# Convolution with residual add: weights in front on ACT's queue with the first residual behind them, the first image as one load in front on SP's queue

## The chip, the cores and the metric

One core of a Trainium2 chip. The time is the device time of the program in microseconds (us), a median over executions; the profile's span, some 2 us shorter, runs from the first to the last instruction of one execution. SP and ACT each issue transfers into a queue of their own; the sixteen DMA engines move them in rows, one row per partition. "Packet records" are the trace's list of single rows and semaphore writes, each with start and duration. TensorE is PE, VectorE is DVE, ScalarE is ACT, GpSimd is POOL, SyncE is SP.

## The reference, cut to what matters

```python
batch, c_in, h, w, c_out, k = 16, 64, 64, 64, 64, 3      # all float32
x_pad = np.pad(x, ((0, 0), (0, 0), (1, 1), (1, 1)))
output[b, co] += weight[co, ci, kh, kw] * x_pad[b, ci, kh:kh+h, kw:kw+w]
return output + residual
```

Image and residual are 16.8 MB each, the weights 0.15 MB, the output 16.8 MB: 50.5 MB have to cross between memory and the core.

## The kernel before

Images are handled in pairs: 128 partitions hold two images of 64 channels, so one load of `x`, one of `residual` and one store move 2 MB, in 128 rows of 16 KB. ACT packs each image into bf16 (two copies), PE convolves it, DVE adds the residual in place (two adds), and SP stores the pair. Three buffers hold images, and every residual pair has its own. The weights are transposed by PE, and DVE and ACT copy them, cast to bf16, into the layout that PE uses.

```python
def load_x(p, engine=nc.sync, cols=slice(0, NPIX)):
    return engine.dma_start(out=xr[p % NXR][:, cols], in_=x_bc[128 * p : 128 * p + 128, cols]).then_inc(
        s_x[p % NXR], 16)
...
# SP's program
for p in range(NPAIR):
    if p >= NXR:
        nc.sync.wait_ge(s_half, 2 * (p - NXR) + 3)     # the image buffer is free
    if p == 0:
        to_the_front(load_x(p, cols=slice(0, NPIX // 2)))   # ahead of the start barrier
        nc.sync.dma_start(out=wraw[:, :], in_=w_rows[:, :]).then_inc(s_w, 16)
    else:
        load_x(p)
    load_ro(p)
for p in range(NEARLY):                                # the first 6 stores
    nc.sync.wait_ge(s_add, 2 * p + 3)
    store(p).then_inc(s_out, 16)
...
# ACT's program
to_the_front(load_x(0, nc.scalar, slice(NPIX // 2, NPIX)))
for n in range(B):
    ...                                                # wait for the pair's load, two copies of image n
    if n == 0:
        nc.scalar.wait_ge(s_wt, 1)                     # the transposes
        ...                                            # four weight copies
...
# the last two stores, after everything above is done
for p in range(NEARLY, NPAIR):
    store(p)
```

`to_the_front` moves a load ahead of the barrier with which the program starts.

## Time and profile before

| | before |
|---|---|
| time, median of 3 (range) | 123.16 us (123.14 to 123.23) |
| span of the profiled execution | 121.2 us |
| busy: PE, DVE, ACT | 72%, 63%, 52% |
| moved, mean rate over the span | 50.48 MB, 417 GB/s |

### The profile page before, as it was taken

The page shows a single profiled execution, that of the slowest core. Times are in us where ns is not written, and L with a number is a line of the kernel's source. Part 1 is how long each engine was busy: PE and PEld are TensorE (multiplying, and loading weights), DVE is VectorE, ACT ScalarE, POOL GpSimd, SP SyncE. Part 2 cuts the span into 40 slices and gives each one's busy share as a digit, 9 for nine tenths or more (in the row PEclk, how much of TensorE's full clock was granted, in tenths as well). Part 3 has the DMA queues.
Part 4 walks back from the last instruction along what each step waited for, and adds up shares of the span by engine and source line. Part 5 has one row for each costly group of instructions (what it writes and reads, how often), then busy time and mean ns, then how long its engine had stood idle before and what let it go on. Part 6 is the DMA issues. An engine that isn't in the chain of part 4 may idle for free.

```text
span 121.2 us, 736 instructions
## 1 busy us (share of the span) xinstructions
PE 87.7 (72%) x389; PEld 10.7 (9%) x105; DVE 76.0 (63%) x40; ACT 63.1 (52%) x37; POOL 2.4 (2%) x16
## 2 busy tenths in 40 slices
PE   0033499999999999999999999999999980000000
PEld 0021001101010101010101010101010100000000
DVE  0005300889898898989889898898989889300000
ACT  4049969938966984993993994896000000000000
POOL 5200000000000000000000000000000000000000
PEclk9999999999999999999999999999999999755555
DMA  6999999999999999999999999999999999999993
GB/s 168 427 444 433 433 433 433 433 427 433 433 427 427 433 433 427 427 433 427 433 433 433 433 433 422 433 389 433 433 433 433 422 433 433 433 433 433 427 433 151
DMA packets 3744, 50.48 MB, mean 417 GB/s; under 512 B 416, under 2 KB 544, under 8 KB 544
## 3 DMA queue, kind: packets, MB, share of 16 engines
q1 hardware_dynamic: 3600, 49.43, 96.3%
q10 hardware_dynamic: 144, 1.05, 2.0%
HBM read 33.70 MB, written 16.78 MB: 417 GB/s over the span
## 4 chain that ended last, share of the span: by engine, by line
PE 71%; DVEq 2%; DVE 2%; issue 0%
PE ps L86 53%; PE ps L85 17%; DVEq L129 2%; DVE ro L201 2%
## 5 line engine op out<-in xcount | busy, mean ns | idle before, releaser
L201 DVE TENSOR_TENSOR ro<-ps,ro 64x2048 f32<-64x2048 f32 x32 | 73.2, 2289 | 17.7 <-PE ps L86 17.2
L86 PE MATMUL ps<-xp,wl 128*128 128x504 bf16 (+1 forms) x288 | 80.0, 388 | 0.2
L173 ACT CAST xp<-xr 64x2048 bf16<-64x2048 f32 x16 | 30.3, 1896 | 19.3 <-DMA xr<-in_x_dram 17.1
L85 PE MATMUL ps<-xp,wl 128*128 128x504 bf16 (+1 forms) x92 | 35.8, 389 | 3.4 <-PEq L222 3.4
L177 ACT CAST xp<-xr 64x2048 bf16<-64x2048 f32 x16 | 30.4, 1897 | 0.4
L85 PEld LDWEIGHTS ps<-xp,wl 128*128 128x128 bf16 x96 | 9.5, 99 | 79.1 <-issue 79.1
L189 DVE CAST wl<-ps 32x192 bf16<-32x192 f32 x8 | 2.8, 348 | 10.4 <-PE ps L214 10.3
L214 PE MATMUL ps<-ident,wraw 128*32 128x128 f32 x9 | 2.1, 412 | 8.1 <-DMA wraw<-in_weight_dram 8.1
L214 PEld LDWEIGHTS ps<-ident,wraw 128*32 128x32 f32 x9 | 1.2, 137 | 8.6 <-issue 8.1
L173 ACT ACT_TABLE_LOAD x1 | 1.3, 1283 | 1.1 <-SPq L129 1.1
L182 ACT CAST wl<-ps 32x192 bf16<-32x192 f32 x4 | 1.2, 306 | 0.0
L160 POOL MEMSET xp<- 64x64 bf16 x4 | 0.6, 147 | 0.2
L159 POOL MEMSET xp<- 64x64 bf16 x4 | 0.6, 145 | 0.2
L148 POOL TENSOR_SCALAR_AFFINE_SELECT ident<-ident 128x128 f32<-128x128 f32 x1 | 0.3, 295 | 0.2 <-POOL ident L146 0.2
L162 POOL MEMSET wl<- 64x192 bf16 x1 | 0.3, 253 | 0.1
L161 POOL MEMSET wl<- 64x192 bf16 x1 | 0.3, 252 | 0.1
L146 POOL MEMSET ident<- 128x128 f32 x1 | 0.2, 205 | 0.7 <-SPq L129 0.7
L257 POOL MEMSET const-uint8-127<- 128x1 uint8 x1 | 0.1, 113 | 0.0
L257 POOL MEMSET const-bfloat16-1.0<- 128x1 bf16 x1 | 0.1, 112 | 0.0
L257 POOL MEMSET const-float32-1.0<- 128x1 f32 x1 | 0.1, 109 | 0.0
L257 POOL MEMSET const-float32-0.0<- 128x1 f32 x1 | 0.1, 104 | 0.2 <-issue 0.2
## 6 DMA issues: line engine op xcount, KB each, us to landing
ro<-in_residual_dram SPq DMA_DIRECT2D x8, 2048.0 KB, 21.9
out_dram<-ro SPq DMA_DIRECT2D x8, 2048.0 KB, 28.2
xr<-in_x_dram SPq DMA_DIRECT2D x7, 2048.0 KB, 17.5
xr<-in_x_dram SPq DMA_DIRECT2D x1, 1024.0 KB, 7.0
xr<-in_x_dram ACTq DMA_DIRECT2D x1, 1024.0 KB, 7.6
wraw<-in_weight_dram SPq DMA_DIRECT2D x1, 144.0 KB, 6.9
```

The lines of the kernel that those rows point to most:

```text
L85: return e.matmul(out=out_, lhsT=lhsT, rhs=rhs, start=start, stop=stop, skip_group_check=True)
L86: return e.add_instruction(mybir.InstMatmult(name=nc.get_next_instruction_name(), engine=PE, ins=[e.lower_ap(rhs), e.lower_ap(lhsT)], outs ...
L129: with tc.tile_critical(no_gpsimd_drain=True):
L159: nc.gpsimd.memset(t[0:64, 0, :], 0.0).then_inc(s_id, 1)
L160: nc.gpsimd.memset(t[64:128, J, :], 0.0).then_inc(s_id, 1)
L173: i = nc.scalar.copy(out=t[64:128, 0:J, :], in_=x4[hp, :, 0, :])
L177: nc.scalar.copy(out=t[0:64, 1 : J + 1, :], in_=x4[hp, :, 1, :]).then_inc(s_pack, 1)
L182: i = nc.scalar.copy(**weight_block(h, *b))
L189: i = nc.vector.tensor_copy(**weight_block(h, *b))
L201: i = nc.vector.tensor_tensor(out=o4[hp, :, par, :], in0=psj[64 * par : 64 * par + 64, :, :], in1=o4[hp, :, par, :], op=ADD)
L214: i = nc.tensor.transpose(out=tp[0:32, t // 3, 128 * (t % 3) : 128 * (t % 3) + 128], in_=wraw3[:, :, t], identity=ident[:, :])
L257: nc = _bacc.Bacc("TRN2", target_bir_lowering=False, num_devices=1)
```

## The change

Its visible intent is to have the weights at PE earlier: they go to the front of ACT's program, ACT casts its weight copies before it packs the first image, the image comes as one load at the front of SP's program, and the first residual leaves SP's queue so that the second image moves up there.

```diff
+    def load_w(rows):
+        return nc.scalar.dma_start(out=wraw[rows, :], in_=w_rows[rows, :]).then_inc(s_w, 16)
...
             if p == 0:
-                to_the_front(load_x(p, cols=slice(0, NPIX // 2)))
-                nc.sync.dma_start(out=wraw[:, :], in_=w_rows[:, :]).then_inc(s_w, 16)
+                to_the_front(load_x(p))
             else:
                 load_x(p)
-            load_ro(p)
+            if p > 0:
+                load_ro(p)
...
-        to_the_front(load_x(0, nc.scalar, slice(NPIX // 2, NPIX)))
+        to_the_front(load_w(slice(0, 112)))
+        load_w(slice(112, 128))
+        load_ro(0, nc.scalar)
+        nc.scalar.wait_ge(s_wt, 1)
+        for b in blocks[4:]:
+            for h in range(2):
+                i = nc.scalar.copy(**weight_block(h, *b))
+        i.then_inc(s_wt, 1)
         for n in range(B):
...
-            if n == 0:
-                nc.scalar.wait_ge(s_wt, 1)
-                for b in blocks[4:]:
-                    for h in range(2):
-                        i = nc.scalar.copy(**weight_block(h, *b))
-                i.then_inc(s_wt, 1)
...
-        nc.tensor.wait_ge(s_w, 16)
+        nc.tensor.wait_ge(s_w, 32)
```

(The waits on the first image's semaphore follow from the number of its loads.)

More of the change, by code (lines that the diff above doesn't have):

```diff
@@ L68, with load_x, load_ro @@
     s_add = sem("s_add")
-    def load_x(p, engine=nc.sync, cols=slice(0, NPIX)):
-        return engine.dma_start(out=xr[p % NXR][:, cols], in_=x_bc[128 * p : 128 * p + 128, cols]).then_inc(
-            s_x[p % NXR], 16
-        )
-    def load_ro(p):
-        nc.sync.dma_start(out=ro[p][:, :], in_=res_bc[128 * p : 128 * p + 128, :]).then_inc(s_r[p], 16)
+    def load_w(rows):
+        return nc.scalar.dma_start(out=wraw[rows, :], in_=w_rows[rows, :]).then_inc(s_w, 16)
+    def load_x(p):
+        return nc.sync.dma_start(out=xr[p % NXR][:, :], in_=x_bc[128 * p : 128 * p + 128, :]).then_inc(s_x[p % NXR], 16)
+    def load_ro(p, engine=nc.sync):
+        engine.dma_start(out=ro[p][:, :], in_=res_bc[128 * p : 128 * p + 128, :]).then_inc(s_r[p], 16)
     def store(p):
@@ L171 @@
             if im == 0:
-                nc.scalar.wait_ge(s_x[p % NXR], 16 * (p // NXR + 1 + (p % NXR == 0)))
+                nc.scalar.wait_ge(s_x[p % NXR], 16 * (p // NXR + 1))
             i = nc.scalar.copy(out=t[64:128, 0:J, :], in_=x4[hp, :, 0, :])
```

## The prediction

> **What bounds the kernel now.** I read four views in this order: the page (is any resource full from start to end?), the stages at the end (what runs last?), the start in order of time (what releases the first convolution?), and the transfer queues in a short stretch near the start (how do two queues share?). First the page: engine PE, the sixteen DMA engines and the bytes, then the chain that ended last.
>
> ```profile
> PE   0033499999999999999999999999999980000000
> ...
> DMA  6999999999999999999999999999999999999993
> ...
> HBM read 33.70 MB, written 16.78 MB: 417 GB/s over the span
> ...
> PE 71%; DVEq 2%; DVE 2%; issue 0%
> ```
>
> The DMA row is full in 38 of 40 slices; PE is idle in the last seven. 50.48 MB at the 434 GB/s of an undisturbed stage is 116.3 us of a 121.2 us span. The chain names PE for 71%, but that chain stops at 104 us; it ended 17 us before the span did. So this kernel is bound by the volume it moves, and compute matters only if it makes a transfer queue run empty. The stages at the end, with the columns span, PE, PEld, DVE, ACT, POOL, clock, DMA share and GB/s, and then the last instructions:
>
> ```profile
> 98.00:104.00 6.00, 1.48 (x7) 0.10 (x1) 5.39 (x3) 0.00 (x0) 0.00 (x0) 1.00 1.01 434
> 104.00:110.00 6.00, 0.00 (x0) 0.00 (x0) 0.13 (x1) 0.00 (x0) 0.00 (x0) 0.54 1.02 434
> 110.00:119.00 9.00, 0.00 (x0) 0.00 (x0) 0.00 (x0) 0.00 (x0) 0.00 (x0) 0.50 1.01 431
> 119.00:121.20 2.20, 0.00 (x0) 0.00 (x0) 0.00 (x0) 0.00 (x0) 0.00 (x0) 0.50 0.09 37
> ```
> ```profile
> 99.52 4.61 DVE L201 TENSOR_TENSOR ro<-ps,ro 64x2048 f32<-64x2048 f32 x2 [0.58 <-PE ps L86]
> 104.42 0.96 SPq L79 DMA_DIRECT2D out_dram<-ro  x2
> ```
>
> The last two stores are issued at 104.42 us, right after the last add, while transfers flow at the full rate on both sides of that moment. In the packet records the last 256 rows of 16 KB (those two stores) begin at 109.57 us. So 5.15 us of older work is queued when they are issued. That is the slack of the whole compute chain, less the time from an issue to its first packet. Now the start:
>
> ```profile
> 7.77 1.90 ACT L173 CAST xp<-xr 64x2048 bf16<-64x2048 f32 x1 [5.41 <-DMA xr<-in_x_dram]
> 8.14 2.08 PE L214 MATMUL ps<-ident,wraw 128*32 128x128 f32 x9 [8.14 <-DMA wraw<-in_weight_dram]
> 10.33 2.90 DVE L189 CAST wl<-ps 32x192 bf16<-32x192 f32 x8 [10.33 <-PE ps L214]
> 11.50 1.26 ACT L182 CAST wl<-ps 32x192 bf16<-32x192 f32 x4
> ...
> 13.66 0.59 PE L85 MATMUL ps<-xp,wl 128*128 128x512 bf16 x1 [3.44 <-PEq L222]
> ```
>
> The weights land at about 8.1, are transposed until 10.2, and DVE's casts of them end at 13.23; 0.43 later PE starts. Image 0 is packed by 11.6. The weights, not the image, release the first convolution. From there PE has practically no idle time until 99.5, so the end of compute moves one for one with PE's start.
>
> Last, how the two queues share: the stretch 2.5 to 6.0 us, when SP's half of the first image (q1) and ACT's half (q10) were both queued, and the landing times of the loads (KB each, us from issue to landing):
>
> ```profile
> q10 hardware_dynamic: 92, 0.75, 50.8%
> q1 hardware_dynamic: 89, 0.73, 49.7%
> ```
> ```profile
> xr<-in_x_dram SPq DMA_DIRECT2D x1, 1024.0 KB, 7.0
> xr<-in_x_dram ACTq DMA_DIRECT2D x1, 1024.0 KB, 7.6
> wraw<-in_weight_dram SPq DMA_DIRECT2D x1, 144.0 KB, 6.9
> ```
>
> 92 packets against 89: the queues take turns, one row each. The single records agree: where SP's queue had come to the weights and ACT's still had 8 KB rows, a 51 ns weight row followed each 309 ns row of the image, and the semaphore write that ends a transfer took a turn too. SP's first packet starts at 1.0 us. ACT's first starts only at 2.67 us, although issued at 0.13.
>
> **What the Trainium skill says.** Three places bear on this. "DMA: Bandwidth & Descriptors", section "Issuing engines are not separate DMA queues": DMAs issued from different engines run on the same 16 engines and interleave, and a second issuer saves only issue time. The trace agrees: two active queues share 434 GB/s. The same page, section "Queues, rings and completion order": each DMA engine round-robins between the queue rows at packet granularity, with a packet of typically 9 to 17 descriptors. The round robin is in this trace; the grouping isn't, a turn here is one row. This decides when the weights land. The same page, section "Latency and other measured facts": first byte of this kind of DMA after about 0.6 us. This trace has 1.0 us on SP's queue and 2.5 us on ACT's, and I use those.
>
> **The change part by part.**
>
> *The first image as one load on SP.* The same 2 MB, in 128 rows of 16 KB in place of 256 of 8 KB. A 16 KB row takes 611 ns in the records, two 8 KB rows 618: 7 ns by 8 rows per DMA engine is 0.06 us saved. The cold start may gain a little too: in the first 2.5 us only 38 packets, 0.31 MB, moved, and larger rows carry more behind each slow first answer. I take 0.1 us in all.
>
> *The weights in front on ACT's queue, 112 rows and then 16.* On each DMA engine that is 7 weight rows, a semaphore write, 1 row, a semaphore write: 10 turns. If ACT's queue again wakes at about 2.7, each engine has two 16 KB rows of the image behind it by about 2.9 (the 38 packets at 2.5 are 1.2 such rows per engine). From there every turn costs a 611 ns image row: 0.66 us for a weight row and its image row. Weight row 7 goes at 2.9 + 6 x 0.66 = 6.9; the image's eighth row ends at 6.8; the semaphore write, row 8 and the last semaphore write need two more rows of the next load in between, to 8.2. A semaphore is seen some 0.4 us after its last write (weights before: last writes at 7.6, transposes at 8.1), and the engines are spread by 0.2. So the image is usable at about 7.5 and the weights at about 8.8, that is 0.65 LATER than now, though they stand first in ACT's program.
>
> *ACT's order.* ACT now casts its weight blocks first, then packs image 0. Transposes start at 8.8; 2.19 (8.14 to 10.33) later, at 11.0, the casts begin: 1.26 for four, then 3.83 for the two packs of image 0: 16.1. DVE's eight casts are done at 13.9, hidden. PE starts at about 16.2 instead of 13.66: 2.5 later. This is the real cost of the order: the pack no longer overlaps the transposes.
>
> *The first residual on ACT's queue.* It now takes turns with the second image load instead of going before it. The second image needs 6 more rows after 8.2, each with a residual row: 6 x 2 x 0.61 = 7.3, landing at about 16 (now 17.8); the residual lands at about 18.5 (now 12.4). Its first reader is DVE's first add, at 21.7 now and some 2.5 later then. Both are hidden.
>
> *The end.* Compute ends at 104.1 + 2.5 = 106.6 and the last stores are issued at 106.9. Their first turn comes at about 109.5, so 2.6 us are left for the start of a transfer, which took 1.0 on SP's queue. Still hidden, with 1.6 us to spare. The other waits have more room: the load of the fourth pair is issued at 19.7 now and some 2.1 later then, while the loads queued ahead of it last until about 32.
>
> Sum: bytes unchanged, queue never empty, start and rows -0.1, compute +2.5 but hidden: 123.16 - 0.1 = 123.05 us.
>
> **The rivals.** (1) The weights really come first: if ACT's queue wakes as early as SP's, or turns hold many rows, they land at 3 to 4 us; the transposes then run by 6.3 (GpSimd's constants are ready at 4.1), the image is packed from 7.5 to 11.3, and PE starts at 11.4, 2.3 earlier. That was probably the intent. Against it: ACT's first packet at 2.67 and the one-row turns. It would still give 123.05, as the last transfers don't depend on it. (2) The delay breaks through at the end: if PE starts over 4 us later, or a late store needs the 2.5 us that ACT's first did, the queue empties before the last stores. With my 2.5 us and such a latency nothing is left, so a further 1 us of delay would show as 1 us: 124. For it: the slack is only 5.15. Against it: the stores are on SP's queue, and SP is already running. (3) The kernel is bound by compute and the start counts in full: 120.8 or 125.7. Against it: the empty PE in the last 17 us beside a full DMA row.
>
> **Range and chances.** Runs of the kernel before span 0.09 us. The cold start gives a few tenths either way, rival (2) a tail upward: 122.5 to 123.8. 2% is 2.46 us. Faster needs fewer bytes or a higher rate, neither in the diff: 0.01. Slower needs a delay of some 6.5 us at PE's start: 0.015. Within: 0.975.
>
> **What would show it.** Right: a full DMA row to about 119; the transposes at 8.5 to 9.2; PE's first convolution at 15.5 to 17, released by ACT's pack; the last stores issued near 107 with full DMA after it. Wrong on the turns: transposes before 6. Wrong on the hiding: a dip in GB/s just before the last two stores flow. If the time moves by over 0.7 us without such a dip, the rate itself has changed, and my account of the bound is incomplete.

## The result, and the profile after

The changed kernel took 123.03 us (median of 6 runs, 122.87 to 123.59), the kernel before 123.15 (6 runs, 123.01 to 123.23). The ratio is 1.000, with a 95% interval of 0.998 to 1.002. The two are the same within a quarter of a per cent.

The page of the changed kernel, its rows for PE and the transfers, its bytes and its chain:

```profile
PE   0006039999999999999999999999999999000000
...
DMA  6999999999999999999999999999999999999993
...
HBM read 33.70 MB, written 16.78 MB: 417 GB/s over the span
...
PE 71%; DVEq 2%; DVE 2%; issue 0%
```

Bytes, rate and the full DMA row are as before. PE's row has moved: it is full from the seventh slice on, where before it was from the sixth, and it ends one slice later. The start in order of time shows by how much:

```profile
9.61 2.08 PE L216 MATMUL ps<-ident,wraw 128*32 128x128 f32 x9 [9.61 <-DMA wraw<-in_weight_dram]
11.72 1.26 ACT L172 CAST wl<-ps 32x192 bf16<-32x192 f32 x4 [8.40 <-PE ps L216]
11.80 2.90 DVE L191 CAST wl<-ps 32x192 bf16<-32x192 f32 x8 [11.80 <-PE ps L216]
13.01 1.90 ACT L181 CAST xp<-xr 64x2048 bf16<-64x2048 f32 x1
14.93 1.90 ACT L185 CAST xp<-xr 64x2048 bf16<-64x2048 f32 x1
...
16.97 0.59 PE L86 MATMUL ps<-xp,wl 128*128 128x512 bf16 x1 [5.29 <-PEq L224]
```

The weights start their transposes at 9.61, 1.5 us LATER than before (8.14), and the first convolution starts at 16.97, 3.3 us later (13.66). The pack of image 0 stands behind the weight copies now; before, it ran beside the transposes. At the end that delay is still almost whole (3.2 us), and still hidden. The stages (columns as in the prediction's) and the last two lines of the timeline:

```profile
104.00:110.00 6.00, 0.00 (x0) 0.00 (x0) 3.29 (x2) 0.00 (x0) 0.00 (x0) 0.79 1.02 434
110.00:119.00 9.00, 0.00 (x0) 0.00 (x0) 0.00 (x0) 0.00 (x0) 0.00 (x0) 0.50 1.01 431
```
```profile
102.71 4.61 DVE L203 TENSOR_TENSOR ro<-ps,ro 64x2048 f32<-64x2048 f32 x2 [0.58 <-PE ps L87]
107.61 0.81 SPq L80 DMA_DIRECT2D out_dram<-ro  x2
```

The last stores are issued at 107.61 instead of 104.42. Their first row begins at 109.41 by the packet records, and the rate is 434 GB/s around it, without a dip. So of the 5.15 us between issue and first row, 3.35 were used up and 1.80 are left.

Why the weights came late, although they stand first on their queue, shows in the queues' share between 3.0 and 6.5 us:

```profile
q1 hardware_dynamic: 82, 1.34, 89.6%
q10 hardware_dynamic: 82, 0.09, 7.8%
```

82 packets from each queue, 1.34 MB against 0.09 MB. The queues take turns row by row, and so every weight row of 1152 bytes (51 ns) waited for a row of 16 KB of the image (611 ns).

### The profile page after: what moved, and what is told of

Its sections match the earlier page's. It is cut to its first block, busy times and chain, and to the rows that moved or that the text cites. A ratio compares the mean times of both kernels' runs of the same rounds, so it can differ in the third digit from the quotient of the medians.

```text
span 121.0 us, 736 instructions
## 1 busy us (share of the span) xinstructions
PE 87.6 (72%) x389; PEld 10.7 (9%) x105; DVE 76.0 (63%) x40; ACT 63.2 (52%) x37; POOL 2.4 (2%) x16
## 4 chain that ended last, share of the span: by engine, by line
PE 71%; DVEq 2%; DVE 2%; issue 0%
PE ps L87 54%; PE ps L86 17%; DVEq L130 2%; DVE ro L203 2%
## 6 DMA issues: line engine op xcount, KB each, us to landing
wraw<-in_weight_dram ACTq DMA_DIRECT2D x1, 126.0 KB, 8.2
```

## The experiments

Theory A: the moved bytes, and the moment at which they begin, set the time; compute is hidden as long as the last stores are issued while older transfers still flow. Rival B: the start of the first convolution counts in full. Rival C: row size or the number of queues changes the rate (in the delay runs C stands for a compute chain that can't reach the end at all). All twelve kernels, with the two already shown, in one table. "First row" is the first packet record of the last two stores. All results are correct, except in the two runs with fewer bytes.

| kernel | PE starts | last stores issued | first row | time, median us | ratio to before, 95% |
|---|---|---|---|---|---|
| before | 13.66 | 104.42 | 109.57 | 123.15 | |
| changed | 16.97 | 107.61 | 109.41 | 123.03 | 1.000 (0.998 to 1.002) |
| p1_image_one_load | 13.91 | 104.66 | 109.39 | 123.14 | 0.999 (0.996 to 1.001) |
| p2_weights_first_on_sp | 15.09 | 104.92 | 109.56 | 123.14 | 1.000 (0.997 to 1.002) |
| p3_pack_before_casts | 15.10 | 105.63 | 109.45 | 123.16 | 0.999 (0.997 to 1.002) |
| p4_residual_on_sp | 16.99 | 107.66 | 109.84 | 123.33 | 1.002 (0.998 to 1.006) |
| q1_image_on_act | 14.65 | 105.68 | 109.81 | 123.06 | 0.999 (0.997 to 1.001) |
| p5_image_after_barrier | 13.22 | 104.26 | 110.64 | 124.06 | 1.007 (1.005 to 1.008) |
| d1_delay | 18.87 | 109.80 | 110.63 | 124.01 | 1.005 (1.003 to 1.008) |
| d2_delay | 20.70 | 110.40 | 111.23 | 125.20 | 1.018 (1.014 to 1.022) |
| l0_less_bytes_before | 13.49 | 103.86 | 104.71 | 118.31 | 0.962 (0.960 to 0.964) |
| l1_less_bytes | 16.95 | 106.84 | 107.68 | 121.19 | 0.984 (0.983 to 0.986) |

**One part alone: the image as one load (from the kernel before).**

```diff
-                to_the_front(load_x(p, cols=slice(0, NPIX // 2)))
+                to_the_front(load_x(p))
-        to_the_front(load_x(0, nc.scalar, slice(NPIX // 2, NPIX)))
```

> The kernel before with one part of the change: the first image as one load on SP, nothing on ACT's queue, weights behind the image on SP. Theory A (the moved bytes set the time, the start is hidden behind them): 122.9 to 123.3 us. Theory B (the start of the first convolution counts in full): 123.4, as PE should start at about 13.9 in place of 13.66 (image rows end at about 7.4, weights seen at 8.3, transposes and casts 5.1, 0.43 to PE). Theory C (row size or the number of queues changes the transfer rate): 0.06 us or more below the kernel before, from fewer and larger rows.

Measured: PE starts at 13.91, as expected, and the time doesn't move. An effect of 0.06 us, as rival C would have it, is below what the interval resolves. So this part explains at most 0.25 us of PE's delay (13.91 for 13.66).

**The weights truly first: on SP's queue ahead of the image (from the changed kernel).**

```diff
+                to_the_front(load_w(slice(0, 112)))            # now issued on SP
                 to_the_front(load_x(p))
-            if p > 0:
-                load_ro(p)
+            load_ro(p)
-        to_the_front(load_w(slice(0, 112)))
-        load_w(slice(112, 128))
-        load_ro(0, nc.scalar)
+        load_w(slice(112, 128), nc.scalar)
```

(All 128 rows in one front load, or both pieces in front, does not compile; I don't know why. So 16 rows had to go behind the barrier.)

> The changed kernel with the 112 weight rows ahead of the image on SP's own queue, the other 16 on ACT's, the residual back on SP. The weights should now really come first: transposes at 4.5 to 5 instead of 9.6, image packed from 8.3 to 12.1, PE starts at about 12.2, 4.8 us before the changed kernel. Theory A: time unchanged, 122.8 to 123.3, last stores issued at about 102.9. Theory B: 118.3. If turns on a DMA engine held many rows, the weights would not move by this much, because they would already have come first.

Half a miss. The 112 rows landed 2.2 us after their issue, but the other 16, issued on ACT at 1.44, had their first row only at 5.5 and landed 6.2 us after their issue. The transposes ran at 7.72 instead of 4.5 to 5, and PE started at 15.09. The time stayed the same with PE 1.9 us earlier than in the changed kernel, which speaks against B, but the early start that I wanted was not reached. Two things follow: both pieces must land, and a load issued just behind a large one on the OTHER queue starts late.

**ACT's order undone (from the changed kernel).**

```diff
-        nc.scalar.wait_ge(s_wt, 1)
-        for b in blocks[4:]: ...                 # weight copies ahead of image 0
...
+            if n == 0:                           # behind the pack of image 0, as before the change
+                nc.scalar.wait_ge(s_wt, 1)
+                for b in blocks[4:]: ...
```

> The changed kernel with ACT's order undone: image 0 is packed before ACT casts its weight blocks. Transposes stay at 9.6; the pack should run from 7.9 to 11.7 beside them, DVE's casts end at 14.7, PE starts at 15.1 instead of 16.97. Theory A: time unchanged, 122.8 to 123.4. Theory B: 121.2.

Measured: transposes at 9.58, PE at 15.10, as expected, and the time the same. So of the changed kernel's 3.3 us delay of PE, ACT's order costs 1.9 and the later weights the other 1.4.

**The first residual back on SP (from the changed kernel).**

```diff
-            if p > 0:
-                load_ro(p)
+            load_ro(p)
-        load_ro(0, nc.scalar)
```

> The changed kernel with the first residual back on SP's queue behind the first image; only the weights on ACT. Transposes should stay at 9.6 and PE at 17.0, as the residual does not take a turn before the weights' last one. The first residual lands at about 12.7, the second image at about 17.6 instead of 16.8. Theory A: 122.8 to 123.4. Theory C (sharing two queues costs rate): below the changed kernel by 0.2 or more.

Measured: transposes at 9.62 and PE at 16.99, as in the changed kernel, so the residual has no part in the delay. The time is the same within its interval. C's 0.2 us below the changed kernel did not show (123.33 against 123.03, of different rounds), but an interval of 0.4% either way could not resolve it.

**The front loads exchanged: image on ACT, weights on SP.**

```diff
-                to_the_front(load_x(p))
+                to_the_front(load_w(slice(0, 112)))            # on SP
+                load_w(slice(112, 128))
-        to_the_front(load_w(slice(0, 112)))
-        load_w(slice(112, 128))
+        to_the_front(load_x(0, nc.scalar))
```

> The changed kernel with the two front loads exchanged: 112 weight rows on SP, the first image on ACT, the other 16 weight rows on SP after the barrier. If ACT's queue wakes late by itself (2.7 to 3.0 us in the traces so far), the image's first row starts there and the transfers lose 1 us or more: 124.0 or above. If it was only kept waiting behind the rows that SP had issued first, the image starts right after the weights, at 1.5 to 1.9, and the time is 123.0 to 123.4. PE's start is 15 to 20 either way, as the second image now takes turns with the first.

This was aimed at an assumption of mine, that ACT's queue by itself wakes at about 2.7 us. The queues between 1.0 and 2.5 us, packets, MB and share:

```profile
q10 hardware_dynamic: 19, 0.31, 90.9%
q1 hardware_dynamic: 128, 0.13, 29.1%
```

ACT's queue (q10) had begun 19 image rows by 2.5 us, its first at 1.42 by the packet records. It doesn't wake late by itself; in the kernels before and after it was kept waiting behind the 128 rows that SP had issued 0.13 us earlier. Here it is the 16 weight rows on SP, issued at about 1.1 behind ACT's image, that begin only at 4.78 us. Why a load waits like this for one on the other queue, and for how long, these runs don't show. The time is unchanged (123.06). PE's start at 14.65 lies just outside the 15 to 20 expected.

**The transfers begin later, PE earlier: the image behind the barrier.**

```diff
-                to_the_front(load_x(p))
+                to_the_front(load_w(slice(0, 112)))            # on SP
+                load_w(slice(112, 128))
+                load_x(p)
-            if p > 0:
-                load_ro(p)
+            load_ro(p)
-        to_the_front(load_w(slice(0, 112)))
-        load_w(slice(112, 128))
-        load_ro(0, nc.scalar)
```

> The changed kernel with all on SP: 112 weight rows in front, then after the start barrier the other 16, the first image, the first residual. Weights are seen by 3, transposes run when GpSimd's constants are ready, 4.1 to 6.2; the image is packed from 8.9 to 12.7, PE starts at about 12.9, 4.1 us before the changed kernel. But the large transfers begin about 1.4 us later, 0.35 of which the weights fill. Theory A (moved bytes and the moment they begin set the time): 123.6 to 124.2, SLOWER though PE starts earlier. Theory B (start of compute counts): 118.9.

The stages of this kernel from 1 to 3 us and one line of its timeline:

```profile
1.00:2.00 1.00, 0.00 (x0) 0.00 (x0) 0.00 (x0) 1.00 (x1) 0.65 (x4) 1.00 0.52 134
2.00:3.00 1.00, 0.00 (x0) 0.00 (x0) 0.00 (x0) 0.25 (x1) 0.73 (x6) 1.00 1.17 243
```
```profile
4.01 2.10 PE L214 MATMUL ps<-ident,wraw 128*32 128x128 f32 x9 [4.01 <-POOL wl L164]
```

The transposes now wait for GpSimd's constants (4.01), not for the weights, and PE starts at 13.22, earlier than in any other full kernel. Yet the time is 124.06, up by 0.7%: the DMA engines are half idle until 2 us, and between 1 and 4 us they moved 0.3 MB less than in the changed kernel (134, 243 and 197 GB/s against 246, 280 and 350), an estimated 0.7 us at 434 GB/s. B would have 119, and is refuted by the sign of the change. A's 123.6 to 124.2 held.

**More delay, one and two copies of 1.9 us ahead of the first pack (from the changed kernel).**

```diff
+            for k in range(1 if n == 0 else 0):                # 2 in the second kernel
+                nc.scalar.copy(out=t[64:128, 0:J, :], in_=x4[hp, :, 0, :]).then_inc(s_slow, 1)
+                nc.scalar.wait_ge(s_slow, k + 1)
             i = nc.scalar.copy(out=t[64:128, 0:J, :], in_=x4[hp, :, 0, :])
```

> The changed kernel with one more copy of 1.9 us on ACT ahead of the first pack: PE starts at 18.9 instead of 16.97, the last stores are issued at 109.55 instead of 107.61. The queued transfers end between 109.4 and 110.2, so the slack of 1.8 us is used up. Theory A (only what goes past the slack shows): the rise is 1.9 - (1.8 - L), with L the time from an issue to its first row on a running SP queue; with L of 1.0 as at the start, 1.1 us, about 124.1; with L near 2, 125. Theory B (all of compute counts): 1.9 us, 124.9. Theory C (compute does not touch the end at all): 123.0. The last rows should begin after a hole in the transfers of about L.

> The same with two such copies: PE starts at 20.9, last stores issued at 111.45. Theory A: once the slack is gone every further microsecond counts in full, 1.9 above the run with one copy: about 126.0 with L of 1.0. Theory B: 126.8. Theory C: 123.0.

The kernel with one copy at the end, stages and last issue:

```profile
107.00:109.50 2.50, 0.00 (x0) 0.00 (x0) 2.47 (x2) 0.00 (x0) 0.00 (x0) 1.00 0.96 413
109.50:110.60 1.10, 0.00 (x0) 0.00 (x0) 0.00 (x1) 0.00 (x0) 0.00 (x0) 0.72 0.01 0
110.60:112.00 1.40, 0.00 (x0) 0.00 (x0) 0.00 (x0) 0.00 (x0) 0.00 (x0) 0.50 1.34 562
```
```profile
109.80 0.81 SPq L81 DMA_DIRECT2D out_dram<-ro  x2
```

This is the hole that the changed kernel just avoids: the queue has run empty, the stores are issued at 109.80, and their first row comes at 110.63, 0.83 later. The time rose to 124.01, near A's 124.1; against the 123.21 of the kernel before in the same rounds the rise is 0.3 to 1.0 us by the interval, a little under A's 1.1, and clear of B's 1.9 and of C's none. With two copies the latency is 0.83 again (110.40 to 111.23) and the hole longer. So the slack that the changed kernel had left in its profiled execution is 1.80 - 0.83 = 0.97 us.

The second run missed its number: 125.2 instead of 126.0, with runs from 124.5 to 126.0. The profiled execution (124.52) was the fastest of its four. In it PE started 1.83 us later than with one copy but ended only 0.6 later. The reason is in PE's first groups of four matmuls, which go at 1.7 us each before they settle at 0.87. The first matmul of the first group at the shorter time, with one copy and then with two:

```profile
25.16 0.38 PE L87 MATMUL ps<-xp,wl 128*128 128x504 bf16 x1
```
```profile
24.03 0.38 PE L87 MATMUL ps<-xp,wl 128*128 128x504 bf16 x1
```

In the profile with two copies that slow phase lasted 3.3 us, in the one with a single copy 5.8, and in the changed kernel 5.2 (from PE's first convolution to the trace's first record of the full clock). Half of the 2.5 us between the first two is the 1.2 that PE caught up. The Trainium skill, "TensorE: Matmul & The Clock Gate", section "Part 1: The HAM clock gate (the "warmup" mystery)", describes such a phase after idleness and says that its length differs from run to run, as the window that PE's activity is measured in runs freely. The traces agree that the length varies: it was 3.3 to 6.0 us over the twelve profiles, and PE's time from first to last convolution varied with it by 1.3 us (84.8 to 86.1). So PE's end, and the slack at the end with it, can differ by about that much for this reason alone. With one trace per kernel, its spread between executions of the same kernel is not shown, nor that it made the other runs of the two kernels slower or faster.

**Fewer bytes: the last residual pair not loaded, in both kernels (the edit to the kernel before; in the changed kernel the condition is `0 < p < NPAIR - 1`).**

```diff
-            load_ro(p)
+            if p < NPAIR - 1:
+                load_ro(p)
+        nc.gpsimd.wait_ge(s_id, 4 + 2 * NXP)
+        nc.gpsimd.memset(ro[NPAIR - 1][:, :], 0.0).then_inc(s_r[NPAIR - 1], 16)
```

> The kernel before, wrong on purpose: the last residual pair is not loaded (GpSimd writes zeros instead), so 2.1 MB or 4.86 us of transfers less. The last stores are still issued at about 104.4; their rows can begin 0.83 later (the delay runs gave 0.83 from issue to first row), at 105.3, in place of 109.57. Theory A: 4.3 us less, 118.9. If the bytes alone counted: 118.3. Theory B (compute counts in full): unchanged, 123.2.

> The changed kernel with the same cut. The last stores are issued at about 107.6, so their rows begin at 108.4 in place of 109.41. Theory A: only 1.0 us less, 122.0, that is 3.1 us or 2.6% slower than the kernel before with the same cut: the 3.2 us of later compute that are hidden in the full kernels show. If the bytes alone counted: 118.2, equal to the other.

Stages near the end of the kernel before, and then of the changed kernel, both without that load:

```profile
103.00:105.00 2.00, 0.00 (x0) 0.00 (x0) 0.56 (x1) 0.00 (x0) 0.00 (x0) 0.62 1.04 442
105.00:107.60 2.60, 0.00 (x0) 0.00 (x0) 0.00 (x0) 0.00 (x0) 0.00 (x0) 0.50 0.95 403
```
```profile
103.00:105.00 2.00, 0.00 (x0) 0.00 (x0) 1.97 (x2) 0.00 (x0) 0.00 (x0) 1.00 0.75 320
105.00:107.60 2.60, 0.00 (x0) 0.00 (x0) 1.55 (x1) 0.00 (x0) 0.00 (x0) 0.69 0.00 0
```

With 4.86 us of transfers less, the kernel before gained 4.8 us (118.31 against 123.08 of the same rounds): bytes set its time. The changed kernel gained only 1.9 (121.19), because its transfers stand still from about 105 to 107.6, until the last stores can be issued. Between these two the changed arrangement is 2.9 us, 2.4% by the medians, slower. Both beat A's own numbers, 118.9 and 122.0, by 0.6 and 0.8: the last stores were issued at 103.86 and 106.84 instead of the 104.4 and 107.6 assumed. In the second kernel PE starts at 16.95, as in the changed kernel, but its slow phase lasted 3.7 us instead of 5.2, and half of that difference is the 0.8. So the delay of PE's start is real and reaches the end; in the full kernels it lies behind queued transfers. This also shows the limit of "bytes set the time": it holds for the kernel before with a margin of 4.3 us (5.15 - 0.83), and for the changed kernel with one of 1.0, both as profiled and so give or take the slow phase of PE.

No version beat the kernel before. The intervals of p1, p2, p3, p4 and q1 all contain 1.

## Why the prediction was right

*The bound.* Right. The transfers fill the same 38 slices, and the time stayed within 0.12 us while PE's start moved by 3.3. Taking bytes away moved the time nearly in full (118.31), and starting the transfers later raised it even with PE earlier (124.06).

*The turns.* Right in kind: one row each (82 to 82), and the weights came later, not earlier, as the prediction said against the change's visible intent. The size was off. The transposes began at 9.61, not 8.8, and outside the 8.5 to 9.2 that I had named. Two terms were too small: the last semaphore writes of the weights were spread over 0.7 us between the DMA engines (8.28 to 8.96 in the packet records) where 0.2 had been allowed; and the last was seen 0.65 later, not 0.4 (the two times that it was taken from differ by 0.5). The first of them came as worked out (8.2). The spread could have been read from the kernel before, where it is 0.6 (7.06 to 7.66). That it comes from the first rows of 16 KB, which took 1.0 to 1.7 us each, is likely but not shown. The second image and the first residual landed at 16.7 and 19.2 for 16 and 18.5, late by as much, and hidden as said.

*The cause of ACT's late first row.* Wrong. I took it as a property of ACT's queue. The number I used for it (2.7) was near what came (2.99), but the exchanged loads show that it was the wait behind SP's load.

*ACT's order.* Right, sized by undoing it: 1.9 us.

*PE's start and the end.* 16.97 for 16.2 and 107.61 for 106.9, both late by about the 0.8 that the weights were. The spare time was then 0.97 instead of 1.6: 0.8 less for the weights and 0.2 more for a latency of 0.83 where I had taken 1.0.

*The 0.1 us saved by larger rows and the start.* Not shown, and in the profiles it goes the other way. By the semaphore writes in the packet records the changed kernel is 0.15 us BEHIND at 76 us. It is 0.21 us ahead only from 81 us on, because the kernel before lost 0.36 us in between, where its loads end and its stores begin. Stages of the kernel before, and then of the changed one:

```profile
75.00:81.00 6.00, 6.00 (x30) 0.64 (x7) 5.39 (x3) 4.69 (x3) 0.00 (x0) 1.00 0.99 399
```
```profile
75.00:81.00 6.00, 6.00 (x30) 0.68 (x7) 5.39 (x3) 4.20 (x3) 0.00 (x0) 1.00 1.02 434
```

399 against 434 GB/s. This loss is no property of the arrangement that I can name: p1, p5, q1 and l0 had it too (0.2 to 0.6 us), p3 had 0.1, and p2, p4, d1, d2 and l1 did not. Its cause stays open. So the hit to 0.02 us is partly luck; the rounds themselves say only that the two kernels are equal within 0.23%.

*The rivals.* (1), the weights first, did not come about; where they did come early (p5) the time showed no gain from it, as the rival's own text said. (2), a break at the end, did not happen, but it was nearer than I gave it: 0.97 us away, and the delay runs show it happening exactly so. The 2.5 us of latency that I feared there did not appear. (3), compute counts in full, was refuted by p5.

## What to carry to other kernels

When the transfer row is full to the end, ask how long the queue still is when the last store is issued: that length less one issue latency is the room in which any change of compute disappears, and a change that hides today can show after the next saving of bytes. A small load beside a large one on another queue is not ahead of it; if the queues take turns by rows, small rows pay one large row each, so put the small load ahead on the SAME queue (112 weight rows ahead of the image landed 2.2 us after their issue). Packing an image while weights are still under way is free work; an order that makes it wait is a real cost, even where the clock doesn't show it.

## What the Trainium skill lacked or had wrong

- "DMA: Bandwidth & Descriptors", section "Queues, rings and completion order": a DMA engine is said to drain typically 9 to 17 descriptors from one ring before it switches. Here it switched after every row, of 1152 bytes, 8 KB or 16 KB (82 packets against 82, 92 against 89; the weight rows of the changed kernel start in batches of 16, some 0.66 us apart), and the semaphore write that ends a transfer took a turn of its own. This contradicts the page only if a row is a single descriptor, which the trace doesn't show.
- The same page, section "Issuing engines are not separate DMA queues": it says that DMAs of several issuers interleave. It does not say that a load issued just behind a large one on the other queue begins late: ACT's first row at 2.67 and 2.99 us after an issue at 0.13; 16 rows on ACT issued at 1.44 began at 5.5; with the loads exchanged, behind 112 small rows, ACT's first row was at 1.42, and SP's 16 rows waited from 1.1 to 4.78.
- The same page, section "Latency and other measured facts": first byte after about 0.6 us. Issue to first row on an empty but running queue was 0.83, 0.83 and 0.84 us here, and 1.0 at the program's start, where the first 16 KB rows then took 1.0 to 1.7 us instead of 0.61.
- "TensorE: Matmul & The Clock Gate", section "Part 1: The HAM clock gate (the "warmup" mystery)": it puts the end of the slow phase at around 4 us, give or take 0.5. That the length varies agrees, but here it was 3.3 to 6.0 us, over 4.5 in nine of the twelve profiles. That this spread made that of d2_delay's times (124.5 to 126.0) is likely but not shown.
- No page has the loss of 0.2 to 0.6 us where loads give way to stores, seen in some profiles and not in others.
